# Hybrid encoder block on one core: first weight load moved to ScalarE's queue, transposes of the identity ahead of the first products, last output tile in two halves

## The chip, the core and the metric

The kernel runs on one core of one Trainium2 chip. TensorE (PE) multiplies, VectorE (DVE) and ScalarE (ACT) work on SBUF and PSUM, GpSimd (POOL) on SBUF only; transfers between HBM and SBUF are issued by SyncE (SP) or by ScalarE on queues of their own. The metric is device microseconds of one execution. Three runs of the kernel before gave 1689.59, 1690.15 and 1693.16 us, median 1690.15.

## What is computed

One encoder layer on two sequences, 2048 tokens and 256 tokens, model width 1024, in fp32. Both are laid end to end as 2304 tokens, 18 tiles of 128.

```
hdn  = rmsnorm(x, norm_pre)
proj = hdn @ w_in                # conv branch, q_lat (384), kv_lat (256), k_pe (32), gates
conv = b_gate * short_conv(c_gate * u) * silu(z_conv)
q    = rmsnorm(q_lat) @ w_uq ; k, v = rmsnorm(kv_lat) @ w_ukv ; rope on part of q and k
attn = softmax(q k^T) v * silu(z_attn)        # 8 heads, no mask
out  = concat(conv, attn) @ w_out
y    = x + rmsnorm(out, norm_post)
```

## The kernel before

Products are made exact enough by splitting each operand into a rounded part (hi) and a rest (lo) and by adding three products, hi hi, hi lo and lo hi (`mm3`, lines 91 to 93). ScalarE makes the rounded part (`split`, line 68; `form`, line 141 for the input), VectorE the rest (lines 69 and 142).

Phase 1 (`phase1`) projects the input. Its first step, lines 316 to 325, brings in the first 384 tokens of x, transposed, and the weights of the latents, in eight slices k of 128 input features each. SyncE issues all of these loads, in program order: x slice 0, the norm's gains g_pre, weights 0, x slice 1, weights 1, x slices 2 and 3 in one transfer, weights 2, weights 3, and so on. For each slice ScalarE scales and rounds x (line 141, `hdn_hi`) and rounds the weights (line 68, `wl_hi`), and VectorE forms `hdn_lo` and `wl_lo`. Then `latents` (line 176) runs over k and, for the first call, over two tiles of 128 tokens: per slice 12 products into four PSUM tiles, six of 384 columns (`pq`) and six of 288 (`pk`). Further tiles, the tokens' norms (`norm_x`) and the other projections follow (`etile`, line 242). In phase 1 the program's planner orders the instructions of an engine from its own costs and due times; from the second phase on the order on PE, DVE, ACT and POOL is the order in which they are written (`manual_schedule`, line 1027).

Ahead of phase 1, line 995 runs one small ScalarE instruction, `ready`, so that ScalarE's table load comes early. The identity matrix is made on GpSimd (line 989); PE uses it to transpose (lines 170 and 223).

Phase 2 makes queries, keys and values from the latents; the attention follows (`Attention`), one head pair and 512 queries at a time. Phase 4 (`Phase4`) is the output projection, one tile of 128 tokens after another in the order 16, 17, 0 to 15. `load` issues the loads of a tile two tiles ahead, `split` cuts it one tile ahead, and `run` (line 950) multiplies it: for each half of 512 columns 16 products with the hi part (line 959) and 8 with the lo part (line 961), all into one PSUM tile of 1024 columns, two banks (`g.wide`, two buffers). When both halves are done, this follows for the whole width:

```
nc.scalar.activation(junk, o, AF.Square, accum_out=sq[:, 0:1])
nc.vector.tensor_tensor(yt, o, g.post, op=ALU.mult)
rstd(g, sq[:, 1:2], sq[:, 0:1], D)
nc.vector.scalar_tensor_tensor(yt, yt, sq[:, 1:2], xt, op0=ALU.mult, op1=ALU.add)
nc.sync.dma_start(self.y[i * P : (i + 1) * P], yt)
```

Both read the same PSUM tile; in the trace the VectorE product of line 967 starts when ScalarE has ended the square of line 966. `rstd` (line 96) is two small GpSimd instructions, lines 99 and 100. The tiles `yt`, `o_cut` and the attention's `p` share a ring of six buffers (tag "p"); `g.narrow` gives PSUM tiles of 512 columns, one bank, and is what the attention uses under the tags "m" and "o".

Of the kernel before, what the change touches and what calls it, by code (L numbers as in the profile page):

```python
# [10 lines left out]
F32 = mybir.dt.float32  # L11
F32R = mybir.dt.float32r
# [3 lines left out]
AF = mybir.ActivationFunctionType  # L16
ALU = mybir.AluOpType
# [4 lines left out]
P = 128  # L22
D = 1024
# [10 lines left out]
LW = QL + KL + ROPE  # L34
CW = 512
EPS = 1e-6
# [23 lines left out]
def f(ap):  # L60
    return ap.bitcast(F32)


def split(nc, hi, lo, src, scale=None):

    whole = f(hi) if hi.dtype == F32R else hi
    if scale is None:
        nc.scalar.activation(hi, src, AF.Copy)
        nc.vector.tensor_tensor(lo, src, whole, op=ALU.subtract)
    else:  # L70
        nc.scalar.activation(hi, src, AF.Copy, scale=scale)
        nc.vector.scalar_tensor_tensor(lo, src, scale, whole, op0=ALU.mult, op1=ALU.subtract)
# [30 lines left out]
def phase1(g, x, x_t, w_e, w_lat, npre, convw, open_phase2):  # L103

    nc, tc = g.nc, g.tc
    with ExitStack() as ctx:
        px = ctx.enter_context(tc.tile_pool(name="p1x", bufs=3, reuse_waits="tile"))
        pl = ctx.enter_context(tc.tile_pool(name="p1l", bufs=2, reuse_waits="tile"))
        pb = ctx.enter_context(tc.tile_pool(name="p1b", bufs=2, reuse_waits="tile"))
        ps = ctx.enter_context(tc.tile_pool(name="p1ps", bufs=2, space=PSUM, reuse_waits="tile"))  # L110
# [5 lines left out]
        wl_hi = pw.tile([P, 8, LW], F32R, name="wl_hi")  # L116
        wl_lo = pw.tile([P, 8, LW], F32R, name="wl_lo")
# [11 lines left out]
        def fetch_t(c, ks):  # L129
            if c not in turned:  # L130
                turned[c] = pw.tile([P, 8, CH], F32, tag="xt", bufs=1, name=f"xt{c}")
                hdn[c] = (
                    px.tile([P, 8, CH], F32R, tag="hdn_hi", bufs=3, name=f"hdn_hi{c}"),
                    px.tile([P, 8, CH], F32R, tag="hdn_lo", bufs=3, name=f"hdn_lo{c}"),
                )
            nc.sync.dma_start(turned[c][:, ks], x_t[:, ks, c * CH : (c + 1) * CH])
# [158 lines left out]
        def conv(hf, j, ci):  # L295
# [17 lines left out]
                nc.gpsimd.tensor_tensor(ys, ys, gt[:, gb : gb + n], op=ALU.mult)  # L313
            nc.sync.dma_start(g.mix[j * P : (j + 1) * P, lo_t:hi_t], y[:, : hi_t - lo_t])

        fetch_t(0, slice(0, 1))
        nc.sync.dma_start(g_pre, npre)
        for k in range(8):
            if k == 1 or k and k % 2 == 0:
                fetch_t(0, slice(k, k + 1 + (k > 1)))  # L320
            wt = pb.tile([P, 8, P], F32R if k % 3 else F32, tag=("w32", "w_hi", "w_lo")[k % 3], name=f"wl{k}")
            wt = f(wt.rearrange("p k e -> p (k e)")[:, :LW])
            nc.sync.dma_start(wt, w_lat[:, k, :])
            form(0, [k])
            split(nc, wl_hi[:, k, :], wl_lo[:, k, :], wt)
        for i in range(3):
            fetch_x(i)
            norm_x(i)
# [3 lines left out]
        n = 0  # L332
        for hf in range(2):
            pend = []
            for c in range(3 * hf, 3 * hf + 3):
                ahead = c + 1 < 3 * hf + 3
# [21 lines left out]
            for j in range(5):  # L358
                if j < 4:
                    edge(hf, j, True)  # L360
                for e in range(4):
                    if n + 1 < 20 * (hf + 1):
                        _, j2, e2 = seq[n + 1]
# [559 lines left out]
class Phase4:  # L923
# [23 lines left out]
        eng = nc.vector if i == T // P - 2 else nc.gpsimd  # L947
        eng.tensor_tensor(ml, m, f(mh), op=ALU.subtract)  # L948

    def run(self, i, ahead):  # L950
        g, nc = self.g, self.g.nc
        _, xt, mh, ml = self.ready.pop(i)
        hi, lo = self.wo
        o = g.wide(f"out{i}")
        for b in range(2):
            w = slice(b * 512, (b + 1) * 512)
            for k in range(8):
                for wk in (hi, lo):
                    nc.tensor.matmul(o[:, w], mh[:, k, :], wk[k // 2][:, k % 2, w], start=k == 0 and wk is hi, stop=False)  # L959
            for k in range(8):  # L960
                nc.tensor.matmul(o[:, w], ml[:, k, :], hi[k // 2][:, k % 2, w], start=False, stop=k == 7)  # L961
        ahead()
        yt = self.at.ps.tile([P, D], F32, tag="p", bufs=6, name=f"yt{i}")
        junk = self.at.ps.tile([P, D], F32, tag="acc", bufs=2, name=f"junko{i}")
        sq = self.at.ps.tile([P, 2], F32, tag="sqo", bufs=2, name=f"sqo{i}")
        nc.scalar.activation(junk, o, AF.Square, accum_out=sq[:, 0:1])  # L966
        nc.vector.tensor_tensor(yt, o, g.post, op=ALU.mult)  # L967
        rstd(g, sq[:, 1:2], sq[:, 0:1], D)
        nc.vector.scalar_tensor_tensor(yt, yt, sq[:, 1:2], xt, op0=ALU.mult, op1=ALU.add)  # L969
        nc.sync.dma_start(self.y[i * P : (i + 1) * P], yt)  # L970


@with_exitstack
def tile_encoder(ctx, tc, x, x_t, w_e, w_lat, w_uq, w_uk, w_uv, w_out, convw, npre, qg, kvg, npost, table, y):
    nc = tc.nc
    g = Ctx()
    g.nc, g.tc = nc, tc
    dram = ctx.enter_context(tc.tile_pool(name="scratch", bufs=1, space=DRAM))
    cpool = ctx.enter_context(tc.tile_pool(name="const", bufs=1))
# [11 lines left out]
    g.exps = cpool.tile([P, 2], F32, name="exps")  # L991
    g.mhalf = cpool.tile([P, 10], F32, name="mhalf")
    nc.gpsimd.memset(g.mhalf, -0.5)

    nc.scalar.activation(cpool.tile([P, 10], F32, name="ready"), g.mhalf, AF.Copy)

    p2 = Phase2(g, table)
    phase1(g, x, x_t, w_e, w_lat, npre, convw, lambda *pools: p2.open(w_uq, w_uk, w_uv, w_lat, npre, qg, kvg, *pools))
# [25 lines left out]
    last = len(p2.chunks) - 1  # L1024
# [45 lines left out]
    p4 = Phase4(g, at, x, (wo[:4], wo[4:]), y)  # L1070
    periods = H * KT
    for p in range(periods):
        at.steps(p)
        for s in (2 * p, 2 * p + 1):
            k, i = divmod(s - 8, 28)
# [5 lines left out]
    tiles = [16, 17, *range(16)]  # L1081
# [4 lines left out]
    n = 2 * H - 1  # L1086
    rest = at.finish(n, n // 4, slice(n % 4 * QB, (n % 4 + 1) * QB))
    for n, i in enumerate(tiles):

        def ahead():  # L1090
            if n + 1 < len(tiles):
                p4.split(tiles[n + 1])
            if n + 2 < len(tiles):
                p4.load(tiles[n + 2])

        p4.run(i, ahead)
        if n < 2:
            for _ in range(4):
                next(rest, None)
# [48 lines left out]
```

## Time and profile before

| what | value |
| --- | --- |
| median of three runs | 1690.15 us |
| the profiled execution, its own time | 1692.56 us |
| its span, first to last instruction | 1690.6 us |
| PE busy | 1647.5 us, 97% of the span |
| DVE, ACT, POOL busy | 750.2, 581.6, 878.5 us |
| granted TensorE clock, mean | 0.994 |

The time of an execution is the span and something around it. Busy times are sums over an engine's instructions; an idle engine costs time only where the end waits for it. PE is the engine whose work fills the span, so one looks for the places where PE stands still, and then for what it waited for there.

### The profile page before, as it was taken

The numbers are of one execution on the slowest core, as the hardware profiler recorded it, in microseconds if no ns is written. First come the engines' busy times: TensorE is split into PE (matmuls) and PEld (weight loads), VectorE is DVE, ScalarE is ACT, GpSimd is POOL, SyncE is SP. The second block draws the span as 40 slices with busy tenths as digits, with TensorE's granted clock in tenths as the row PEclk, the third lists the DMA queues.
The fourth block names the chain that finished last, engine by engine and source line by source line (L and its number), as shares of the span: only waits on it lengthen the run. The fifth ranks groups of instructions, "written<-read, shape, count | busy, mean of one in ns | idle before, by whom it ended". The sixth has DMA issues, their size and how long they took to land. (4 is left out here: it accounts for less than half of the span.)

```text
span 1690.6 us, 22364 instructions
## 1 busy us (share of the span) xinstructions
PE 1647.5 (97%) x8870; PEld 1115.8 (66%) x8870; DVE 750.2 (44%) x1125; ACT 581.6 (34%) x804; POOL 878.5 (52%) x637
## 2 busy tenths in 40 slices
PE   8999999999999999978999999999999999999998
PEld 8999999999999997556333333333333333378886
DVE  4333332423474222337556665666666666132122
ACT  7521111452222122411444444444444444512211
POOL 3321221033342112145788988989899898942222
PEclk9999999999999999989999999999999999999999
DMA  8921112364324116378011131113111210034443
GB/s 292 273 87 60 52 52 83 112 165 118 114 94 137 55 62 167 106 194 214 13 32 32 44 85 41 44 32 94 31 45 32 69 44 13 26 105 144 149 141 109
DMA packets 141741, 158.97 MB, mean 94 GB/s; under 512 B 33842, under 2 KB 118116, under 8 KB 141636
## 3 DMA queue, kind: packets, MB, share of 16 engines
q1 hardware_dynamic: 122916, 148.11, 29.3%
q10 hardware_dynamic: 18720, 9.44, 1.9%
q8 instruction: 69, 1.13, 0.3%
q14 instruction: 36, 0.29, 0.1%
HBM read 109.72 MB, written 41.89 MB: 90 GB/s over the span
## 5 line engine op out<-in xcount | busy, mean ns | idle before, releaser
L809 POOL TENSOR_TENSOR acc<-acc,p 128x1024 f32<-128x1024 f32 x224 | 527.9, 2357 | 60.6 <-ACT p L799 50.5
L753 DVE TENSOR_REDUCE mx<-m 128x1 f32<-128x512 f32 x512 | 337.7, 691 | 237.2 <-PE m L752 237.1
L799 ACT ACTIVATE p<-s,exps 128x1024 f32<-128x1024 f32 x256 | 271.4, 1111 | 348.2 <-PE s L794 348.2
L91 PE MATMUL o<-hdn_hi,whi 128*128 128x384 f32 x960 | 323.5, 337 | 0.0
L92 PE MATMUL o<-hdn_lo,whi 128*128 128x384 f32 x960 | 322.7, 336 | 0.0
L93 PE MATMUL o<-hdn_hi,wlo 128*128 128x384 f32 x960 | 322.6, 336 | 0.0
L789 PE MATMUL s<-q,k 128*128 128x512 f16 x1024 | 302.7, 381 | 1.0 <-ACT p L799 1.0
L920 PE MATMUL o<-p,v 128*64 128x512 f32 x1024 | 247.7, 605 | 0.0
L789 PEld LDWEIGHTS <-k 128*128 128x128 f16 x1024 | 90.7, 98 | 190.8 <-issue 101.4
L752 PE MATMUL m<-k,q 96*128 96x512 f16 x512 | 195.4, 382 | 14.4 <-DVE mx L753 8.7
L91 PEld LDWEIGHTS o<-hdn_hi,whi 128*128 128x128 f32 x960 | 180.5, 188 | 0.5
L92 PEld LDWEIGHTS o<-hdn_lo,whi 128*128 128x128 f32 x960 | 180.5, 188 | 0.0
L93 PEld LDWEIGHTS o<-hdn_hi,wlo 128*128 128x128 f32 x960 | 180.5, 188 | 0.0
L920 PEld LDWEIGHTS o<-p,v 128*64 128x64 f32 x1024 | 62.2, 136 | 127.5 <-issue 127.0
L959 PE MATMUL out<-wo,o_cut 128*128 128x512 f32 x576 | 140.4, 396 | 0.0
L959 PEld LDWEIGHTS out<-wo,o_cut 128*128 128x128 f32 x576 | 108.0, 188 | 27.7 <-issue 0.8
L948 POOL TENSOR_TENSOR o_cut<-o_raw,o_cut 128x1024 fp32r<-128x1024 f32 x17 | 40.8, 2399 | 118.3 <-ACT o_cut L945 118.3
L279 POOL TENSOR_TENSOR gt<-gt,z 128x384 f32<-128x384 f32 x24 | 28.7, 1197 | 141.1 <-ACT z L278 141.1
L236 ACT ACTIVATE whi<-w 128x1024 fp32r<-128x1024 f32 x40 | 42.2, 1058 | 172.8 <-PE o L92 159.6
L752 PEld LDWEIGHTS <-q 96*128 96x128 f16 x512 | 49.6, 97 | 63.9 <-issue 6.2
L967 DVE TENSOR_TENSOR yt<-out,g_post 128x1024 f32<-128x1024 f32 x18 | 22.0, 1224 | 150.7 <-ACT junko L966 141.7
L271 POOL TENSOR_TENSOR cu<-cu,rb 128x384 f32<-128x384 f32 (+2 forms) x28 | 27.5, 987 | 112.4 <-DVE cu L270 112.4
(230 smaller groups left out, 2016.4 us busy)
## 6 DMA issues: line engine op xcount, KB each, us to landing
w<-in_w_e_dram SPq DMA_DIRECT2D x40, 512.0 KB, 3.5
x<-in_x_dram SPq DMA_DIRECT2D x18, 512.0 KB, 6.8
o_raw<-mix_s SPq DMA_DIRECT2D x18, 512.0 KB, 4.8
o_raw<-in_x_dram SPq DMA_DIRECT2D x18, 512.0 KB, 5.6
out_dram<-yt SPq DMA_DIRECT2D x18, 512.0 KB, 6.2
q<-qn_s SPq DMA_DIRECT2D x64, 128.0 KB, 2.7
xt<-in_x_t_dram SPq DMA_DIRECT2D x5, 1536.0 KB, 8.3
k<-kn_s SPq DMA_DIRECT2D x12, 512.0 KB, 7.1
```

The lines of the kernel that those rows point to most:

```text
L91: nc.tensor.matmul(out, sh, mh, start=first and i == 0, stop=False)
L92: nc.tensor.matmul(out, sh, ml, start=False, stop=False)
L93: nc.tensor.matmul(out, sl, mh, start=False, stop=last and i == n - 1)
L236: nc.scalar.activation(hi, w, AF.Copy)
L752: nc.tensor.matmul(m, q[:DQK, i, 2, b * P : (b + 1) * P], k[:DQK, i, 1, c * 512 : (c + 1) * 512], start=True, stop=True)
L753: nc.vector.reduce_max(mx[:, u, c : c + 1], m, axis=AX.X)
L789: nc.tensor.matmul(o, k[:, ki, x, ks], q[:, qi, x, :], start=x == 0, stop=False)
L799: nc.scalar.activation(p, o, AF.Exp, scale=g.exps[:, 0:1])
L809: nc.gpsimd.tensor_tensor(self.acc[key], self.acc[key], first, op=ALU.add)
L920: nc.tensor.matmul(self.o[n][i * DV : (i + 1) * DV], g.v[:, kt, h * DV : (h + 1) * DV], p[:, i * QB : (i + 1) * QB], start=kt == 0, stop=k ...
L948: eng.tensor_tensor(ml, m, f(mh), op=ALU.subtract)
L959: nc.tensor.matmul(o[:, w], mh[:, k, :], wk[k // 2][:, k % 2, w], start=k == 0 and wk is hi, stop=False)
```

## The change

Three edits. In phase 1 the load of weight slice 0 is issued by ScalarE's queue, as its first instruction, ahead of SyncE's loads; the other seven stay on SyncE. The `ready` instruction moves from ahead of phase 1 to behind that issue, and eight PE transposes of the identity into two rotating PSUM tiles are added ahead of the first products. In phase 4 the last tile in order (tile 15) is computed in two PSUM tiles of 512 columns, each with its own square, product with `g.post` and, at the end, its own final VectorE instruction and store, the first half by SyncE, the second by ScalarE. In that tile the epsilon is added to half 0's sum, and half 1's sum, half 0's and the factor 1/1024 go into one GpSimd instruction. For every tile, `yt`, `junk` and `sq` are allocated ahead of the products, and `sq` is three columns wide.

```
--- before.py
+++ after.py
@@ -313,16 +313,29 @@
                 nc.gpsimd.tensor_tensor(ys, ys, gt[:, gb : gb + n], op=ALU.mult)
             nc.sync.dma_start(g.mix[j * P : (j + 1) * P, lo_t:hi_t], y[:, : hi_t - lo_t])
+
+        wts = {}
+
+        def fetch_wl(k, queue):
+            wt = pb.tile([P, 8, P], F32R if k % 3 else F32, tag=("w32", "w_hi", "w_lo")[k % 3], name=f"wl{k}")
+            wts[k] = f(wt.rearrange("p k e -> p (k e)")[:, :LW])
+            queue.dma_start(wts[k], w_lat[:, k, :])
+
+        fetch_wl(0, nc.scalar)
         fetch_t(0, slice(0, 1))
         nc.sync.dma_start(g_pre, npre)
+
+        nc.scalar.activation(pl.tile([P, 10], F32, name="ready", bufs=1), g.mhalf, AF.Copy)
+        for i in range(8):
+            turn = ps.tile([P, 3, P], F32, tag="tl", name=f"turn{i}")[:, 0]
+            nc.tensor.transpose(turn, g.ident, g.ident)
         for k in range(8):
             if k == 1 or k and k % 2 == 0:
                 fetch_t(0, slice(k, k + 1 + (k > 1)))
-            wt = pb.tile([P, 8, P], F32R if k % 3 else F32, tag=("w32", "w_hi", "w_lo")[k % 3], name=f"wl{k}")
-            wt = f(wt.rearrange("p k e -> p (k e)")[:, :LW])
-            nc.sync.dma_start(wt, w_lat[:, k, :])
+            if k:
+                fetch_wl(k, nc.sync)
             form(0, [k])
-            split(nc, wl_hi[:, k, :], wl_lo[:, k, :], wt)
+            split(nc, wl_hi[:, k, :], wl_lo[:, k, :], wts.pop(k))
         for i in range(3):
             fetch_x(i)
             norm_x(i)
@@ -947,27 +960,50 @@
         eng = nc.vector if i == T // P - 2 else nc.gpsimd
         eng.tensor_tensor(ml, m, f(mh), op=ALU.subtract)
-    def run(self, i, ahead):
-        g, nc = self.g, self.g.nc
+    def products(self, o, b, mh, ml):
+
+        nc = self.g.nc
+        hi, lo = self.wo
+        w = slice(b * 512, (b + 1) * 512)
+        for k in range(8):
+            for wk in (hi, lo):
+                nc.tensor.matmul(o, mh[:, k, :], wk[k // 2][:, k % 2, w], start=k == 0 and wk is hi, stop=False)
+        for k in range(8):
+            nc.tensor.matmul(o, ml[:, k, :], hi[k // 2][:, k % 2, w], start=False, stop=k == 7)
+
+    def run(self, i, ahead, last):
+        g, nc, ps = self.g, self.g.nc, self.at.ps
         _, xt, mh, ml = self.ready.pop(i)
-        hi, lo = self.wo
+        yt = ps.tile([P, D], F32, tag="p", bufs=6, name=f"yt{i}")
+        junk = ps.tile([P, D], F32, tag="acc", bufs=2, name=f"junko{i}")
+        sq = ps.tile([P, 3], F32, tag="sqo", bufs=2, name=f"sqo{i}")
+        rows = self.y[i * P : (i + 1) * P]
+        if last:
+
+            for b in range(2):
+                w = slice(b * 512, (b + 1) * 512)
+                o = g.narrow(f"out{i}_{b}", "mo"[b])
+                self.products(o, b, mh, ml)
+                nc.scalar.activation(junk[:, w], o, AF.Square, accum_out=sq[:, b : b + 1])
+                nc.vector.tensor_tensor(yt[:, w], o, g.post[:, w], op=ALU.mult)
+                if b == 0:
+                    nc.gpsimd.tensor_scalar(sq[:, 0:1], sq[:, 0:1], 1.0, D * EPS, op0=ALU.mult, op1=ALU.add)
+            nc.gpsimd.tensor_scalar(sq[:, 2:3], sq[:, 1:2], sq[:, 0:1], 1.0 / D, op0=ALU.add, op1=ALU.mult)
+            nc.gpsimd.tensor_tensor(sq[:, 2:3], sq[:, 2:3], g.mhalf[:, :1], op=ALU.pow)
+            for b, queue in enumerate((nc.sync, nc.scalar)):
+                w = slice(b * 512, (b + 1) * 512)
+                nc.vector.scalar_tensor_tensor(yt[:, w], yt[:, w], sq[:, 2:3], xt[:, w], op0=ALU.mult, op1=ALU.add)
+                queue.dma_start(rows[:, w], yt[:, w])
+            return
         o = g.wide(f"out{i}")
         for b in range(2):
-            w = slice(b * 512, (b + 1) * 512)
-            for k in range(8):
-                for wk in (hi, lo):
-                    nc.tensor.matmul(o[:, w], mh[:, k, :], wk[k // 2][:, k % 2, w], start=k == 0 and wk is hi, stop=False)
-            for k in range(8):
-                nc.tensor.matmul(o[:, w], ml[:, k, :], hi[k // 2][:, k % 2, w], start=False, stop=k == 7)
+            self.products(o[:, b * 512 : (b + 1) * 512], b, mh, ml)
         ahead()
-        yt = self.at.ps.tile([P, D], F32, tag="p", bufs=6, name=f"yt{i}")
-        junk = self.at.ps.tile([P, D], F32, tag="acc", bufs=2, name=f"junko{i}")
-        sq = self.at.ps.tile([P, 2], F32, tag="sqo", bufs=2, name=f"sqo{i}")
         nc.scalar.activation(junk, o, AF.Square, accum_out=sq[:, 0:1])
         nc.vector.tensor_tensor(yt, o, g.post, op=ALU.mult)
         rstd(g, sq[:, 1:2], sq[:, 0:1], D)
         nc.vector.scalar_tensor_tensor(yt, yt, sq[:, 1:2], xt, op0=ALU.mult, op1=ALU.add)
-        nc.sync.dma_start(self.y[i * P : (i + 1) * P], yt)
+        nc.sync.dma_start(rows, yt)
 @with_exitstack
@@ -992,8 +1028,6 @@
     g.mhalf = cpool.tile([P, 10], F32, name="mhalf")
     nc.gpsimd.memset(g.mhalf, -0.5)
-    nc.scalar.activation(cpool.tile([P, 10], F32, name="ready"), g.mhalf, AF.Copy)
-
     p2 = Phase2(g, table)
     phase1(g, x, x_t, w_e, w_lat, npre, convw, lambda *pools: p2.open(w_uq, w_uk, w_uv, w_lat, npre, qg, kvg, *pools))
     pool = lambda name, **kw: ctx.enter_context(tc.tile_pool(name=name, reuse_waits="tile", **kw))
@@ -1093,7 +1127,7 @@
             if n + 2 < len(tiles):
                 p4.load(tiles[n + 2])
-        p4.run(i, ahead)
+        p4.run(i, ahead, n + 1 == len(tiles))
         if n < 2:
             for _ in range(4):
                 next(rest, None)
```

## Rows read from the trace of the kernel before

**Rows 1.** Page, part 1: each engine's busy us (share of the span) xinstructions

```profile
PE 1647.5 (97%) x8870; PEld 1115.8 (66%) x8870; DVE 750.2 (44%) x1125; ACT 581.6 (34%) x804; POOL 878.5 (52%) x637
```

**Rows 2.** PE's waits: waiter, what it waited for, us in total, times, longest

```profile
PE qr L91 <- DMA lt_q<-lat_s: 6.2, 1, 6.2
PE pq L91 <- ACT wl_hi L68: 6.0, 1, 6.0
```

**Rows 3.** Timeline, first 12 us: start, us, engine, line, operation, idle before it

```profile
1.07 0.29 POOL masks.py:199 TENSOR_SCALAR_AFFINE_SELECT ident<-ident 128x128 f32<-128x128 f32 x1
1.18 0.42 SPq L317 DMA_DIRECT2D g_pre<-in_npre_dram  x1
1.64 0.43 SPq L323 DMA_DIRECT2D wl<-in_w_lat_dram  x1
...
3.44 0.61 ACT L141 ACTIVATE hdn_hi<-xt,g_pre 128x384 fp32r<-128x384 f32 x1 [1.22 <-DMA g_pre<-in_npre_dram]
...
5.19 0.76 ACT L68 ACTIVATE wl_hi<-wl 128x672 fp32r<-128x672 f32 x1 [1.13 <-DMA wl<-in_w_lat_dram]
...
6.00 0.69 PE L91 MATMUL pq<-wl_hi,hdn_hi 128*128 128x384 f32 x1 [6.00 <-ACT wl_hi L68]
...
8.99 1.12 ACT L141 ACTIVATE hdn_hi<-xt,g_pre 128x384 fp32r<-128x384 f32 x2 [1.41 <-DMA xt<-in_x_t_dram]
...
9.54 0.51 PE L91 MATMUL pq<-wl_hi,hdn_hi 128*128 128x384 f32 x1
...
10.07 0.34 PE L93 MATMUL pq<-wl_hi,hdn_lo 128*128 128x384 f32 x1
...
10.80 1.64 DVE L69 TENSOR_TENSOR wl_lo<-wl,wl_hi 128x672 fp32r<-128x672 f32 x2
...
11.74 0.42 PE L92 MATMUL pq<-wl_lo,hdn_hi 128*128 128x384 f32 x1
```

**Rows 4.** Windows: us, busy us of each engine, granted clock, DMA share, GB/s

```profile
2.50:4.00 1.50, 0.00 (x0) 0.00 (x0) 0.00 (x0) 0.56 (x1) 0.00 (x0) 1.00 0.79 176
4.00:5.50 1.50, 0.00 (x0) 0.00 (x0) 0.62 (x1) 0.37 (x2) 0.00 (x0) 1.00 1.02 371
```

**Rows 5.** The identity's users: count, ns min/median/max, first and last start us

```profile
L223 PE MATMUL tk<-ident,kpl x18: 270/272/273, 37.9 to 417.7; 128*32 128x128 f32 x18
```

**Rows 6.** Timeline of the last output tile, from PE's last eight products

```profile
1681.17 2.03 PE L961 MATMUL out<-wo,o_cut 128*128 128x512 f32 x8
1683.29 1.02 ACT L966 ACTIVATE junko<-out 128x1024 f32<-128x1024 f32 x1 [10.09 <-issue]
1684.21 0.19 ACT L966 ACTIVATION_READ_ACCUMULATOR junko<-out 128x1 f32 x1
1684.44 1.22 DVE L967 TENSOR_TENSOR yt<-out,g_post 128x1024 f32<-128x1024 f32 x1 [8.60 <-ACT junko L966]
...
1684.77 0.54 POOL L100 TENSOR_TENSOR sqo<-sqo,mhalf 128x1 f32<-128x1 f32 x1
1685.75 1.28 DVE L969 SCALAR_TENSOR_TENSOR yt<-yt,sqo,o_raw 128x1024 f32<-128x1024 f32 x1
```

**Rows 7.** Timeline of SyncE's queue after 1682 us: the last store's issue

```profile
1687.06 0.33 SPq L970 DMA_DIRECT2D out_dram<-yt  x1
```

**Rows 8.** Groups by shape, 512 columns from PSUM: busy us, mean ns, idle before

```profile
L820 ACT ACTIVATE rsum<-r 128x512 f32<-128x512 f32 x16 | 9.6, 597 | 11.5 <-PE r L818 11.5
...
L828 DVE TENSOR_TENSOR res<-o,gate 128x512 f32<-128x512 f32 x16 | 11.1, 692 | 48.0 <-POOL gate L825 48.0
```

**Rows 9.** DMA issues after 1685 us: KB each, median us from issue to landing

```profile
out_dram<-yt SPq DMA_DIRECT2D x1, 512.0 KB, 2.6
```

**Rows 10.** DMA issues of the whole span: stores of 128 rows of 2 KB

```profile
mix_s<-res SPq DMA_DIRECT2D x16, 256.0 KB, 2.0
```

**Rows 11.** DMA issues of the whole span: stores on ScalarE's queue

```profile
qn_s<-sq ACTq DMA_DIRECT2D x9, 512.0 KB, 5.6
```

**Rows 12.** Windows: a stretch in the projection stage with a lower granted clock

```profile
740.00:760.00 20.00, 13.97 (x87) 9.98 (x88) 5.64 (x10) 2.17 (x3) 8.29 (x7) 0.74 0.63 181
```

## The prediction

> **What bounds the kernel now.** The page's first part comes first: TensorE (PE) is busy 97% of the span [rows 1], so a change counts only where PE stands still or comes after the last product. Then PE's waits [rows 2]: one of the largest is 6.0 us, ahead of the very first product; the 6.2 us one lies in the projection stage, on data that this stage itself makes, so it moves along with whatever comes before. The change touches the first stretch and the one after the last product. Behind it PE has no row of waiting that comes from the start, so I let what is won there travel to the end.
>
> In the first stretch [rows 3] follow one input slice k = 0..7 at a time: two loads (x, then weights), ScalarE rounds each, VectorE forms the rests, PE multiplies. ScalarE sat idle 1.13 us for the first weights and began at 5.19; PE began at 6.00. Later it sat idle 1.41 us for x slices 2 and 3, until 8.99; VectorE had the weight rests of 2 and 3 from 10.80 on, about 11.62 for slice 2 (half of 1.64), and the first product that needs them starts at 11.74 and takes 0.42 instead of the 0.34 of its shape. So PE arrives at slice 2 only just before its data. That is the important reading: a PE that starts earlier, or runs faster in slices 0 and 1, waits there.
>
> In the last stretch [rows 6, 7] PE ends at 1683.20 (1681.17 + 2.03); the square on ScalarE, its accumulator, the product with g.post, the final VectorE instruction and the store follow each other, and the span ends at 1690.6: 7.4 us with PE idle.
>
> **The change, part by part.**
>
> *First weights on ScalarE's queue.* The issue at 1.64 leaves SP; each SP load behind it moves up by the spacing of two issues, 1.64 - 1.18 = 0.46 us [rows 3]. On ScalarE the issue stands ahead of the table load and the `ready` instruction; at SP's 0.43 it pushes them to about 2.7, and ScalarE waits for g_pre until 3.44 anyway, so that costs nothing; without that cover it would cost 0.43. What is won is how much earlier slices 2 and 3 land, since they hold PE next: 0.46, plus the 0.08 that PE lost at slice 2, about 0.5 us. How the byte stream reacts is not shown, so it is bounded. From 2.5 to 4.0 us the DMAs moved 176 GB/s, right after that 371 [rows 4]. If the early issue fills this hole completely, 1.5 x (371 - 176) / 371 = 0.79 us are won, 0.87 with the 0.08. If the engines, already 0.79 busy there, only swap one load for another, it is nothing. A loss is excluded as far as I see: the bytes ahead of slice 2 are the same ones. I take 0.5, nearest to the issue spacing, and keep 0 and 0.87.
>
> The row speaks for 0.79, since the engines moved less than half of what they could. The Trainium skill ("DMA: Bandwidth & Descriptors", section "Issuing engines are not separate DMA queues") says that transfers issued by different engines interleave on the same 16 DMA engines, and that issuing from several saves only the sequencer's issue time. By that rule the end of 0.79 falls away and the sum below stays as it is; no stretch of this trace has two queues loading weights at once.
>
> *Transposes of the identity ahead of the first products.* Eight, on an otherwise idle PE, from about 1.4 us (the identity's last instruction on GpSimd). One transpose took 0.27 us at the full clock [rows 5]; doubled for the half clock and laid end to end, 8 x 0.54 = 4.3 us, until 5.7. The first product could come at about 5.2 instead of 6.0, so they could delay it to 5.7, which is still early enough for slice 2. What they may bring is the clock: the granted clock prints 1.00 from the start, yet a 384-column product took 0.51 us at 9.54 and 0.34 at 10.07 [rows 3], so I read 1.2 GHz for PE's first 4 us of work and 2.4 after it. Twelve products ran before 9.54; at 0.17 each that is 2.0 us at most, in front of the wait at slice 2, which swallows it: with data 0.46 earlier, PE gets 0.54 whether it comes to slice 2 early or very early. So I put the transposes at zero, with slice 2 as the cover; if the loads came much earlier they would be worth up to the difference.
>
> Rows 3 can't say whether transposes raise the clock. The Trainium skill ("TensorE: Matmul & The Clock Gate", Part 4, "PE-mode transpose") says that the full clock does not engage for them, since they don't count as busy in the same way. By that rule the start is worth some 0.4 instead of 0.5, since a cold PE starting at 5.7 comes 0.1 late to slice 2 (6.00 to 11.74 now took 5.7 us), and the sum would be 1.5 instead of 1.6.
>
> *Moved tiles.* yt, junk and sq are now taken ahead of the products in every output tile. yt still follows the yt of two tiles before in its ring of six, and the loads follow those of two tiles before, which they wait for anyway through the raw buffers: nothing.
>
> *The last tile in halves.* Each half has its own PSUM bank. Half 0 ends about 5.6 us before PE does, so its square, product and the small GpSimd step lie under half 1's products. For half 1 the chain is: square on 512 columns 0.60 [rows 8] from 1683.29, its accumulator read out from 1683.79 to 1683.98 (overlapping by 0.10 as now); then the two GpSimd steps, 0.91 from the end of the accumulator to the end of the power (1684.40 to 1685.31 now [rows 6]), to about 1684.9. VectorE's product, 0.69 for 512 columns [rows 8], runs beside it from 1684.0 to 1684.7. So GpSimd now releases the last instruction, where the long product did before. Then two final instructions on VectorE: 1.28 for 1024 columns; with the slope of (1.22 - 0.69)/512 columns one half is 0.75. With 0.1 for the handoff: 1685.0 to 1685.75, and 1686.5. The last store is issued at 1686.5 instead of 1687.06, and is 256 KB: such a store took 2.0 us to land [rows 10], the last one of 512 KB 2.6 [rows 9]. So 0.55 + 0.6, about 1.1 us. Nothing is queued behind the new issue on ScalarE. Upper end 1.4 (handoff and the pointer operand cost nothing, the two stores overlap well); lower end 0, where the store on ScalarE's queue takes 1.1 us longer to land.
>
> **Sum.** 0.5 + 1.1 = 1.6 us. The profiled execution took 1692.56 with a span of 1690.6 (1.96 around it); it would become 1690.96. The median of three, 1690.15, is 2.41 lower than the profiled execution; the same 1.6 off it gives 1688.55, rounded to 1688.6.
>
> **Rivals.**
> - *The loads only swap places.* Start worth 0, end 1.1: 1689.05. For it: the engines are 0.79 busy in the hole. Against: their rate there is under half.
> - *Both ends at their best.* 0.87 + 1.4 = 2.3: 1687.9. The hole is filled, and the clock is up when slice 2 is there. This is also the case in which the transposes pay.
> - *The last store lands late (slower).* Place: after 1686.5. Stores on ScalarE's queue took a median of 5.6 us to land [rows 11], though larger in number of packets and beside other traffic. At 5.6 instead of 2.0 the end is 3.6 later: 1690.15 - 1.6 + 3.6 = 1692.15, slower than before; it decides from a landing of 3.6 us on (2.0 + 1.6). Against it: at the end nothing else is on the DMAs.
> - *Another clock dip in the middle.* Between 740 and 760 the granted clock was 0.74 with 13.97 us of PE work [rows 12], after PE's wait of 6.2 us. One more such dip costs (1 - 0.74) x 13.97 = 3.6 us, one less gives as much: 1692.2 or 1685.0. The four executions shown of the same program already span 1689.59 to 1693.16, 3.57 us, about that price; a shift of half a microsecond can land in either.
> - *The change does nothing at the end* (the halves wait for each other in another way) is inside the bounds of the forecast: 1689.65.
>
> **How the numbers follow.** Forecast 0.45 (its own range 1687.7 to 1689.7), loads swap 0.2, both best 0.14, late store 0.07, another dip 0.14. The range takes in the first three with the scatter of runs, and most of the dip upward: 1686.4 to 1691.4. About 0.2%, 3.4 us, is what a measurement of this kernel can tell from no change. Faster by more needs a time under 1686.77: the best case with luck, or a dip less: 0.08. Slower by more needs one over 1693.53: 0.05. The rest, 0.87, is the same.
>
> **What would show it.** In the changed trace: the weights' first ScalarE instruction before 5.19; PE's first product between 5.1 and 5.8; x slices 2 and 3 about 0.46 before 8.99; the second product of slice 2 about 0.5 before 11.74, with a wait ahead of it if the clock was up. At the end, PE's last product to the end of the span 6.3 us instead of 7.4, GpSimd's power as what VectorE waits for, and the last store landing in 2.0. The forecast is wrong if slice 2's products start at 11.7 again, if PE shows a new wait between 12 and 640 us, if the store on ScalarE's queue takes over 3 us, or if the stretch from 640 to 860 us changes by more than 1 us.

## The result, and the profile after

The change makes the kernel slower: a median of 1702.36 us over six runs (1698.16 to 1703.24), beside 1692.8 over six runs of the kernel before (1689.59 to 1694.47). The ratio is 1.0055, with a 95% interval of 1.004 to 1.0071. The forecast of 1688.6 and its whole range (up to 1691.4) lie below that. The prediction gave a clear loss a chance of 0.05, and it came by a way that none of its rivals names.

The profiled execution after took 1703.24 us with a span of 1701.4, 10.8 more than before. The page's first part shows where to look:

```profile
PE 1660.4 (98%) x8878; PEld 1127.1 (66%) x8878; DVE 752.2 (44%) x1127; ACT 582.1 (34%) x806; POOL 880.4 (52%) x638
```

Beside [rows 1] PE has eight instructions more, the transposes, and is busy 12.9 us longer. So PE did not come to stand still; it worked longer on the same products. PE's waits in the changed kernel say the same, since they answer to [rows 2] with nearly the same sizes and have no new large row:

```profile
PE qr L91 <- DMA lt_q<-lat_s: 6.4, 1, 6.4
PE pq L91 <- ACT hdn_hi L141: 5.9, 1, 5.9
```

Starts of the same instructions in both traces cut the 10.8 us into stages. The second projection (`etile`: 2880 products `o<-hdn`, the inputs moving past the weights) began at 75.53 us before and at 77.44 after, and its last product at 645.10 and 656.76. The output products began at 1478.65 and 1490.49. From PE's end to the span's end it is 7.40 us before and 6.39 after. So between these two executions the start lost 1.9 us, the stretch of the second projection 9.75, all between there and PE's end 0.2, and the end won 1.0.

**The start.** The timeline of the changed kernel, in the columns of [rows 3]:

```profile
0.72 0.39 ACTq L322 DMA_DIRECT2D wl<-in_w_lat_dram  x1
...
4.63 0.76 ACT L68 ACTIVATE wl_hi<-wl 128x672 fp32r<-128x672 f32 x1 [1.97 <-DMA wl<-in_w_lat_dram]
...
5.30 1.11 ACT L141 ACTIVATE hdn_hi<-xt,g_pre 128x384 fp32r<-128x384 f32 x2
...
5.95 0.69 PE L91 MATMUL pq<-wl_hi,hdn_hi 128*128 128x384 f32 x1 [5.95 <-ACT hdn_hi L141]
...
7.46 1.12 ACT L141 ACTIVATE hdn_hi<-xt,g_pre 128x384 fp32r<-128x384 f32 x2 [0.29 <-DMA xt<-in_x_t_dram]
...
9.75 2.23 PE L331 MATMUL turn<-ident 128*128 128x128 f32 x8
...
11.63 0.62 PE L91 MATMUL pq<-wl_hi,hdn_hi 128*128 128x384 f32 x1
...
12.09 0.34 PE L92 MATMUL pq<-wl_lo,hdn_hi 128*128 128x384 f32 x1
```

The weights are rounded at 4.63 instead of 5.19, but the first product starts at 5.95 instead of 6.00, because x slice 0 now comes second on ScalarE. The eight transposes stand *behind* the twelve products of slice 0, from 9.75 to 11.63, although the program text has them ahead: in phase 1 the planner orders PE. And the first product at the short duration of 0.34 us comes at 12.09, where it came at 10.07 before.

The loads: windows of the changed kernel, columns as in [rows 4], then DMA issues of its first 6 us (KB each, median us from issue to landing), and last the rows of g_pre and of x slice 0 in that view of the kernel before.

```profile
2.50:4.00 1.50, 0.00 (x0) 0.00 (x0) 0.00 (x0) 0.15 (x1) 0.00 (x0) 1.00 0.91 326
4.00:5.50 1.50, 0.00 (x0) 0.00 (x0) 0.08 (x1) 0.87 (x2) 0.00 (x0) 1.00 1.04 335
```

```profile
wl<-in_w_lat_dram ACTq DMA_DIRECT2D x1, 336.0 KB, 3.9
xt<-in_x_t_dram SPq DMA_DIRECT2D x1, 192.0 KB, 4.1
g_pre<-in_npre_dram SPq DMA_DIRECT2D x1, 4.0 KB, 3.8
```

```profile
g_pre<-in_npre_dram SPq DMA_DIRECT2D x1, 4.0 KB, 2.2
xt<-in_x_t_dram SPq DMA_DIRECT2D x1, 192.0 KB, 2.5
```

The hole was filled, 326 instead of 176 GB/s, and x slices 2 and 3 were rounded from 7.46 on instead of 8.99. Still the first product got almost nothing. Its three loads traded places: the weights came earlier, but x slice 0, issued at 0.72 in both kernels, took 4.1 us instead of 2.5, and the 4 KB of gains, issued at 1.18 in both, took 3.8 instead of 2.2. They landed at about 4.6, 4.8 and 5.0; then ScalarE rounds the weights first and x slice 0 from 5.30 on. The Trainium skill ("DMA: Bandwidth & Descriptors", section "Issuing engines are not separate DMA queues") says that transfers of different issuers interleave on the same engines; these rows agree, and show the price for the small load.

**The second projection.** Windows inside it, before and then after (busy us and instructions of PE, PEld, DVE, ACT, POOL; granted clock, DMA share, GB/s):

```profile
200.00:340.00 140.00, 140.00 (x820) 140.00 (x819) 48.10 (x69) 34.10 (x58) 22.65 (x29) 1.00 0.23 79
400.00:600.00 200.00, 199.31 (x1180) 198.26 (x1179) 96.18 (x181) 44.26 (x66) 65.44 (x69) 1.00 0.33 105
```

```profile
200.00:340.00 140.00, 140.00 (x800) 140.00 (x799) 45.85 (x65) 29.34 (x46) 21.69 (x24) 1.00 0.23 78
400.00:600.00 200.00, 199.35 (x1159) 198.31 (x1158) 95.08 (x178) 43.74 (x68) 60.90 (x69) 1.00 0.34 104
```

PE is as busy in both, at a granted clock of 1.00, yet it does 800 products instead of 820, and 1159 instead of 1180. From start to start of neighbouring products (gaps over 0.4 us left out) the mean is 173.7 ns before and 177.0 after: 3.3 ns x 2880 = 9.5 us. That is nearly the whole loss.

**The end** of the changed kernel, against [rows 6, 7], and its two last stores, against [rows 9]:

```profile
1693.03 2.02 PE L972 MATMUL out<-wo,o_cut 128*128 128x512 f32 x8
1695.09 0.60 ACT L987 ACTIVATE junko<-out 128x512 f32<-128x512 f32 x1 [4.86 <-PE out L972]
...
1696.30 0.54 POOL L992 TENSOR_TENSOR sqo<-sqo,mhalf 128x1 f32<-128x1 f32 x1
1696.87 1.42 DVE L995 SCALAR_TENSOR_TENSOR yt<-yt,sqo,o_raw 128x512 f32<-128x512 f32 x2 [0.37 <-POOL sqo L992]
...
1698.32 0.36 ACTq L996 DMA_DIRECT2D out_dram<-yt  x1
```

```profile
out_dram<-yt ACTq DMA_DIRECT2D x1, 256.0 KB, 2.0
```

GpSimd's power now releases the last VectorE instructions, 1.82 us behind PE's end (1695.05); the last store is issued 3.27 us behind it and lands in 2.0.

### The profile page after: what moved, and what is told of

Same layout as the page of the kernel before. It is cut to its first block, busy times and chain, and to the rows that moved or that the text cites. A ratio compares the mean times of both kernels' runs of the same rounds, so it can differ in the third digit from the quotient of the medians.

```text
span 1701.4 us, 22382 instructions
## 1 busy us (share of the span) xinstructions
PE 1660.4 (98%) x8878; PEld 1127.1 (66%) x8878; DVE 752.2 (44%) x1127; ACT 582.1 (34%) x806; POOL 880.4 (52%) x638
```

## Experiments

### What made the second projection slower

The `ready` tile of ten floats (40 bytes, 64 as laid out) left the constant pool, which lies ahead of most other tiles in SBUF, for a pool of phase 1. Everything that follows the constant pool thereby lies 64 bytes lower in a partition: the inputs `hdn`, for one. The weights `whi` and `wlo` lie behind phase 1's pool and keep their place. The first pair of runs moves only that tile, in the one kernel back and in the other out.

```
a_ready_const: after.py
-        nc.scalar.activation(pl.tile([P, 10], F32, name="ready", bufs=1), g.mhalf, AF.Copy)
+        nc.scalar.activation(g.ready, g.mhalf, AF.Copy)
...
+    g.ready = cpool.tile([P, 10], F32, name="ready")
b_ready_moved: before.py
-    nc.scalar.activation(cpool.tile([P, 10], F32, name="ready"), g.mhalf, AF.Copy)
+        nc.scalar.activation(pl.tile([P, 10], F32, name="ready", bufs=1), g.mhalf, AF.Copy)
```

> The changed kernel, with the 40-byte tile of the `ready` instruction back in the constant pool, so that every SBUF address after it is the one of the kernel before (the input tiles hdn 64 bytes higher than in the changed kernel); nothing else differs, the PSUM banks and the eight transposes stay as changed. Theory A (the address of the moving operand hdn sets the pace of the 2880 products of line 91 to 93 in the second projection): spacing from 177.0 back to 173.4 to 173.7 ns, that stretch 9.5 us shorter, time about 9.5 us under the changed kernel, within 3 us of the kernel before. Theory B (the other PSUM banks that the transposes leave to the products): spacing stays at 177, time as changed, some 10 us over before. In both the first stretch still carries the transposes' 2 us and the end its 1 us gain.

> The kernel before, with only the `ready` tile taken from the first phase's pool instead of the constant pool: hdn and all that follows lies 64 bytes lower, PSUM banks, order of loads and products as before. Theory A: spacing 177.0 ns, the stretch 9.5 us longer, time about 9.5 us over before. Theory B: spacing 173.7, time as before within 2 us.

Measured: with the tile back in place the whole change stands at a ratio of 0.9993 (0.9982 to 1.0005); the move alone, with nothing else of the change, at 1.0065 (1.0045 to 1.0085). Spacing in the second projection is 173.7 ns in the first and 177.0 in the second. The same window, of the kernel before with the tile moved:

```profile
400.00:600.00 200.00, 199.35 (x1159) 198.31 (x1158) 93.58 (x177) 42.85 (x64) 61.95 (x69) 1.00 0.34 104
```

The 1159 products are those of the changed kernel. The first run keeps the other PSUM banks that the transposes leave to the products, so these are not the cause. So the slower pace is the moved tile's, whole. Next: is it the inputs' own place or their place against the weights?

```
c_weights_moved: after.py; i_w64: before.py (with 32, 48, 64 floats: i_w128, i_w192, i_w256)
+        pad = pb.tile([P, 16], F32, name="pad", bufs=1)
+        nc.gpsimd.memset(pad[:, :16], 0.0)
         g_pre = pl.tile([P, 8], F32, name="g_pre", bufs=1)
h_ready32, h_ready128: before.py, n = 8 or 32
-    nc.scalar.activation(cpool.tile([P, 10], F32, name="ready"), g.mhalf, AF.Copy)
+    nc.scalar.activation(cpool.tile([P, n], F32, name="ready")[:, :8], g.mhalf[:, :8], AF.Copy)
```

> The changed kernel with a 64-byte tile ahead of the pool that holds the weights of the second projection: their addresses rise by 64, hdn stays where the change put it. If the distance between weights and input counts (modulo 128 bytes it is then as in the kernel before): spacing 173.4 to 173.7 ns and some 9.5 us less than the changed kernel. If the input's own address counts: 177.0 ns, time as changed. In between: both count.

> The kernel before with the weights alone moved up by 64 bytes (96 modulo 128), hdn where it was (64 modulo 128): the distance differs from the kernel before by 64, as it does in the changed kernel. Distance alone: 177 ns and some 9.5 us slower. The input's own place alone: 173.4, time as before.

> The kernel before with the `ready` tile cut to 32 bytes, so that the input hdn and the weights w_hi and w_lo both lie 32 bytes lower (hdn at 32 modulo 128, weights at 0); their distance is that of the kernel before. If only the distance between the two operands sets the pace: 173.4 ns in both halves of the second projection. If the input's own place matters: another spacing, between 173.4 and 177.

> The kernel before with the `ready` tile widened to 128 bytes: hdn and weights both 64 bytes higher (hdn at 0 modulo 128, as in the changed kernel, weights at 96, as in c_weights_moved); same distance as in the kernel before. Distance alone: 173.4 in both halves. hdn at 0 modulo 128 alone: 177 in both. As c_weights_moved did: 176.4 in the first half of the second projection and 173.4 in the second; then the place, and not the transposes, makes that difference.

Moving the weights alone by 64 bytes (i_w64), with the inputs where they were, gives 177.0 ns and 1696.96 us, beside 1691.94 for the kernel before on the same chip. Moving inputs and weights together, by 32 bytes down or 64 up, leaves 173.7 ns. So the pace hangs on where the two lie against each other. Shifting the weights up by 64 bytes as well (c) did not restore it; that makes the distance 128 bytes less than before, and gave 176.5 ns in the first half of the stage and 173.9 in the second, where the kernel before has 173.5 and 173.9 (1694.85 us, before's median beside it 1689.96). Windows of that run:

```profile
200.00:340.00 140.00, 140.00 (x801) 140.00 (x800) 46.59 (x66) 30.36 (x48) 21.74 (x24) 1.00 0.23 78
400.00:600.00 200.00, 199.31 (x1180) 198.26 (x1179) 94.78 (x181) 44.23 (x67) 62.44 (x70) 1.00 0.34 105
```

A surprise stood in h_ready32, at 1682.05 us beside 1691.94. Its second projection is as before, but in the output projection, where `o_cut` moves with the constant pool and `wo` does not, PE does more. The same window, before and then h_ready32:

```profile
1500.00:1660.00 160.00, 160.00 (x688) 128.79 (x687) 36.69 (x30) 31.52 (x43) 45.58 (x44) 1.00 0.44 144
```

```profile
1500.00:1660.00 160.00, 160.00 (x708) 132.48 (x707) 39.13 (x32) 30.80 (x43) 45.89 (x45) 1.00 0.45 146
```

Spacing of the 512-column products is 227.1 ns against 233.7: 6.6 x 864 = 5.7 us. With 64 bytes of shift either way it was 233.7 (after) and 234.7 (h_ready128). The distance between operands matters there too.

More distances, by moving the weights alone; the last three start from the version j below, whose inputs and weights lie 32 bytes lower. The runs c, h and i, and d, e and g below, are single executions, and their times scatter by more than the pace explains (i_w128 1695.04, i_w192 1691.81, i_w256 1691.07 us, beside 1690.36 for the kernel before); what is compared is the spacing in their traces.

> The kernel before with the weights of the second projection 128 bytes higher, inputs unmoved. Theory A, the pace hangs on the distance between the operands modulo 256 bytes: the distance is that of the run in which inputs and weights were moved apart by 128 bytes, so 176.4 ns in the first half and 173.4 in the second, mean 175.2, 4.3 us more in the second projection than before. Theory B, modulo 128: as before, 173.7. Output products 233.7 ns on both, their operands do not move.

> The kernel before with the weights of the second projection 192 bytes higher, inputs unmoved. Theory A (distance modulo 256) has seen no run at this distance: between 173.4 and 177 ns, no number of its own. Theory B (modulo 128): as the run with the weights moved by 64 bytes, 177.0 ns, 9.5 us more.

> The kernel before with the weights of the second projection 256 bytes higher, inputs unmoved. Theories A and B (distance modulo 256 or 128): as before, mean 173.7 ns. Theory C, the place of the weights itself counts and no pattern repeats: some other pace, between 173.4 and 177 ns or outside.

```
l_w32, l_w96, l_w160: j_halves_ready32, n = 8, 24, 40
+        pad = pb.tile([P, n], F32, name="pad", bufs=1)
+        nc.gpsimd.memset(pad[:, :8], 0.0)
         g_pre = pl.tile([P, 8], F32, name="g_pre", bufs=1)
```

> The version with halves and a 32-byte `ready` tile, with the weights of the second projection 32 bytes higher, so that inputs minus weights is 128 modulo 256. Theory A, an even multiple of 32 is faster as in the output products (2.8% there): some 168.8 ns, 14 us less in the second projection, ratio to before near 0.988. Theory B, only 64 bytes off is slow and everything else runs at 173.7: 173.7 ns, ratio 0.996.

> As the run before it, weights 96 bytes higher, inputs minus weights 64 modulo 256. Theory A: some 168.8 ns, ratio near 0.988. Theory B: between the slow 177.0 at 96 and the 173.7 to 175.2 at 32: 174 to 177 ns, ratio 0.997 to 1.002.

> As the run before it, weights 160 bytes higher, inputs minus weights 0 modulo 256, the distance that the output products have where they are fast. Theory A: some 168.8 ns, ratio near 0.988. Theory B: 173.7 to 175 ns, ratio 0.996 to 0.999. Theory C, only 0 is fast: 168.8 ns here, and not in the two runs before it.

Mean spacing in the second projection, by the place of inputs minus weights modulo 256 bytes (places as laid out in the compiled kernels: before, `hdn_hi0` at 17216 and `whi0` at 140704):

```
  0   l_w160                          173.7 ns
 32   c_weights_moved, i_w128         175.2, 173.9
 64   l_w96                           173.7
 96   after, b_ready_moved, i_w64     177.0, 177.0, 177.0
128   l_w32                           176.2
160   before, a, h_ready32, h_ready128, j, i_w256   173.7
224   i_w192                          173.7
```

i_w256 is back at the value of before, so a shift of 256 changes nothing, and i_w192 at 173.7 against i_w64 at 177.0 rules out a pattern of 128. That an even multiple of 32 bytes is faster (theory A of the last three) fell: 64 and 0 are no faster than 160, and 128 is slow:

```profile
400.00:600.00 200.00, 199.35 (x1166) 198.30 (x1165) 93.77 (x180) 43.03 (x65) 60.59 (x64) 1.00 0.34 105
```

(l_w32, ratio 0.9994, 0.9984 to 1.0003: its slow second projection eats what its output products and halves win.) Distance alone is not the whole law either: at 32 two kernels differ, 175.2 and 173.9, with other absolute places. These two means are mixtures. The stage runs through 40 weight tiles, the buffers of the inputs lie a multiple of 256 bytes from one another, and so do those of the weights, so the distance modulo 256 is the same for each. Yet c runs its weight tiles 3 to 20 at the slow pace of the changed kernel and the others at that of before, and i_w128 only the 1st, 22nd and 27th at the slow one. So at this distance both paces occur, in one execution and at the same places. What in the chip makes some distances slow, and what chooses there, stays open. The Trainium skill ("SBUF — State Buffer", section "Who interferes with whom") gives PE two independent read ports, for the moving operand and for weight loads, and says that PE never waits on anyone. Read so, no distance should matter; the runs differ from that by 1.9% (177.0 against 173.7), and the measurement decides.

### What the start lost

```
f_turn_first: a_ready_const
+            last_turn = nc.tensor.transpose(turn, g.ident, g.ident)
...
+                        with tc.issue_after(last_turn.ins):
+                            done = latents(tiles)
d_no_turn: a_ready_const
-        for i in range(8):
-            turn = ps.tile([P, 3, P], F32, tag="tl", name=f"turn{i}")[:, 0]
-            nc.tensor.transpose(turn, g.ident, g.ident)
g_x_before_w: f_turn_first
+                made[c, k] = nc.scalar.activation(
...
+            with tc.issue_after(made[0, k].ins):
                 split(nc, wl_hi[:, k, :], wl_lo[:, k, :], wts.pop(k))
```

> The changed kernel with the old addresses (as a_ready_const), and the eight transposes put in front of the first products on TensorE by an order edge, which is what the change says it does. If my prediction's slice-2 argument holds: transposes from about 1.4 us on, first product between 5.5 and 6.0, no transposes later, the second projection starts about 0.5 us before the 75.53 of the kernel before (2.4 us before the changed kernel's 77.44), and the time is about 1.5 us under before. If transposes raise the clock, 384-column products take 0.34 us from the first one on and a wait of about 1 us stands ahead of slice 2; if they don't, the first products take 0.5 us as before.

> The changed kernel with `ready` in its old pool and the eight transposes left out; the weights' load stays on ScalarE's queue. Theory A, the transposes are what the start lost: PE held 2.2 us by them behind slice 0 and they give no clock, so the first 12 products run straight on, the second projection begins 1.4 to 2.2 us before 76.96 (at 74.8 to 75.6), the span is about 1686. Theory B, the order of ScalarE's work is what the start lost (the wait for a rounded x slice near 34 us): the 2.2 us only move into that wait, the second projection begins at 76.7 to 77.3 again, the span stays near 1687.5. On either theory the products of the second projection stay at 173.7 ns.

> The transposes first on PE (as in the run with the transposes first) and, in each slice, ScalarE's rounding of x ahead of its rounding of the weights. Theory A, ScalarE's order made the wait of 1.3 to 1.45 us near 34 us: with the old order it is gone, the second projection begins at 75.5 to 76.0 instead of 77.26, the first product near 5.5. Theory B, the wait comes from the loads: it stays, and the second projection begins at 77.0 to 77.5. Products of the second projection at 173.7 ns on either.

Without the transposes (d, 1689.6 us beside 1692.79) the second projection begins at 75.55, against 76.96 with them (a) and 75.53 before. Taken as they stand, these three traces say that the transposes cost 1.4 us and that the earlier weights were worth nothing. But the start scatters: in the 13 traces of kernels whose first loads and products are ordered as before, the second projection begins between 74.80 (l_w160) and 76.43 (e_halves). With the transposes behind slice 0 it begins at 77.44, 77.01 (c), 76.96 (a) and, with the best addresses, 75.91 (k, below), where the kernels with the same `ready` tile and the old start have 74.80 to 75.73. What is certain is that the transposes hold PE for 1.3 us (k) to 1.9 us (the changed kernel) and that no wait behind them takes it back; the price of 1.4 is that of one pair. The timeline of d:

```profile
7.56 1.12 ACT L141 ACTIVATE hdn_hi<-xt,g_pre 128x384 fp32r<-128x384 f32 x2 [0.52 <-DMA xt<-in_x_t_dram]
...
9.37 1.68 DVE L69 TENSOR_TENSOR wl_lo<-wl,wl_hi 128x672 fp32r<-128x672 f32 x2
...
10.62 0.29 PE L91 MATMUL pk<-wl_hi,hdn_hi 128*128 128x288 f32 x1
...
11.95 0.34 PE L91 MATMUL pq<-wl_hi,hdn_hi 128*128 128x384 f32 x1
```

Slice 2's data are 1.4 us earlier than before, its first product at 11.95 is later (11.56 before), and no wait stands ahead of it. Not the data but PE's slow first products set that time: full pace (0.29 for 288 columns) comes at 10.62, where it came at 10.07 before.

With the transposes held first (f, ratio 0.9993, 0.9983 to 1.0002), its timeline shows what they do for the clock:

```profile
1.42 2.29 PE L331 MATMUL turn<-ident 128*128 128x128 f32 x8 [1.42 <-POOL ident masks.py:199]
6.10 0.69 PE L91 MATMUL pq<-wl_hi,hdn_hi 128*128 128x384 f32 x1 [2.39 <-ACT hdn_hi L141]
...
8.86 0.52 PE L93 MATMUL pq<-wl_hi,hdn_lo 128*128 128x384 f32 x1
...
10.15 0.34 PE L92 MATMUL pq<-wl_lo,hdn_hi 128*128 128x384 f32 x1
```

The first products still last 0.52 us and 0.34 only from 10.15 on, 1.2 and 2.4 GHz as I read them, since the granted clock prints 1.00 throughout. From the first product to full pace it is 4.1 us here and 3.6 in g, which has the transposes first too; it is 4.7 in d, and in the 13 traces with the old order anything from 3.0 (h_ready128) to 6.1 (h_ready32), without any transpose. The 6.1 of the changed kernel lies at the edge of that. So whatever transposes ahead or between the products change in the time to full pace, it does not stand out from this scatter. The Trainium skill ("TensorE: Matmul & The Clock Gate", Part 4, "PE-mode transpose") says the full clock does not engage for them. The products of f and g, slow after eight transposes and an idle stretch, agree with that; but in k full pace came ahead of the transposes and they ran at it, and in c it came while only transposes ran, behind twelve products. Rows of k, then durations of the transposes (ns, least, median, most) in the changed kernel and in k:

```profile
9.25 0.29 PE L92 MATMUL pk<-wl_lo,hdn_hi 128*128 128x288 f32 x1
...
9.52 1.54 PE L331 MATMUL turn<-ident 128*128 128x128 f32 x8
10.81 0.42 PE L91 MATMUL pq<-wl_hi,hdn_hi 128*128 128x384 f32 x1
```

```profile
L331 PE MATMUL turn<-ident x8: 415/421/475, 9.7 to 11.6; 128*128 128x128 f32 x8
```

```profile
L331 PE MATMUL turn<-ident x8: 271/272/328, 9.5 to 10.8; 128*128 128x128 f32 x8
```

Then f loses 1.3 us of its own, at a wait that neither before nor a has, and g, where ScalarE rounds x ahead of the weights as before, keeps it. PE's waits in g, up to 80 us:

```profile
PE pq L91 <- ACT wl_hi L68: 2.4, 1, 2.4
...
PE pq L91 <- ACT hdn_hi L141: 1.4, 1, 1.4
```

Both begin the second projection at 77.3. In g's timeline the wait ends at 35.60, for a rounded slice which ScalarE begins at 34.93, behind its latents' work (lines 200, 201, 71) and norms; before, the same four slices begin at 33.17. So both theories of g fell: the loads are innocent and so is ScalarE's first order; the planner, given one more order edge, queued ScalarE otherwise 25 us later. g also shows the price of the early weights for x: slice 0, here first again, is rounded at 4.76 instead of 3.44, having waited for g_pre:

```profile
ACT hdn_hi L141 <- DMA g_pre<-in_npre_dram: 2.1, 1, 2.1
```

### The halves alone, and a better kernel

e_halves is the kernel before with the change's `products`, `run` and the call with `last`, and nothing at the start. j_halves_ready32 adds h_ready32's edit; k_after_ready32 is a_ready_const with `ready` eight floats wide.

> The kernel before with the last tile in halves (and the moved allocations) and nothing else. From PE's last product's end to the end of the span 6.4 us instead of 7.4 (the changed kernel has 6.4), the second projection at 173.4 ns, the first products at 6.0 and the second projection from 75.5 as before; the moved tiles change nothing. Rival: the moved allocations or the halves cost something before the last tile, and the stretch from 1478 us to PE's end grows over 205.1 us.

> The kernel before with the last tile in halves and the `ready` tile cut from 40 to 32 bytes, nothing at the start. If the pace of the output products follows the distance of their two operands in SBUF: 227 ns instead of 233.7 in 864 products, 5.7 us, and 1.0 us from the halves: ratio to before 0.996 (6.7 us off some 1690). If the earlier single run at 1682.05 was mostly chance in the stretch from 646 to 800 us: output products at 233.7 ns again, ratio 0.9994.

> The whole change, with the `ready` tile back in its old pool and 32 bytes wide. If distance alone sets the pace: second projection at 173.7 ns, output products at 227 ns, 5.7 us under the run with `ready` back in place (ratio 0.9993 there): ratio 0.996. The start, 1.4 us later than before, is in that ratio. If the 32 bytes did not set the pace: 0.9993 again.

e took 1688.06 beside 1691.94, with 6.39 us from PE's end to the span's end as in the changed kernel, 1.0 less than before. (Its first product came at 6.75 and its second projection at 76.43, not at 6.0 and 75.5; in h_ready128, whose start is that of before, the first product came at 6.83: the start's own scatter.) j stands at 0.9964 (0.995 to 0.9978), k at 0.9953 (0.9939 to 0.9968), and l_w96, the same as j with its weights 96 bytes on, at 0.9952 (0.9935 to 0.997) and 1682.18 us: the lowest median of those that ran more than once, though the three intervals overlap; l_w160 stands at 0.9965 (0.9952 to 0.9978). All beat the kernel before by some 6 to 8 us, and the changed kernel by more; 5.7 of it comes by eight bytes less in one tile that nothing reads.

## Why the prediction was wrong

- **"Moved tiles ... nothing"** is the step that failed. The term listed `yt`, `junk` and `sq` and asked who waits for whom. The one tile that counted, `ready`, appears in the prediction only as an instruction on ScalarE; that its pool shifts every tile behind it was not asked. In its place: 64 bytes, 9.5 us, shown by a and b. No rival had it; the likely cases differed at the two ends alone, so the range could not hold it. The test "a new wait between 12 and 640 us" pointed at the right stretch but at the wrong sign of trouble: no wait, but a pace.
- **"Transposes ... from about 1.4 us on ... at zero, with slice 2 as the cover"** failed twice. The planner put them behind slice 0, where they hold PE for 1.3 to 1.9 us (1.4 us in a against d); and the cover did not exist. Their size was off too: the 0.27 us of [rows 5] is a duration at the full clock, and at half pace the duration is 0.42 to 0.48, but they follow each other every 0.27 us. The eight of f took 2.3 us, not 4.3.
- **"PE arrives at slice 2 only just before its data"** was the false reading under the start's 0.5 us. d brought the data 1.4 us earlier and PE came no sooner. PE's slow first products bound that stretch, as d shows; the two happened to meet in [rows 3]. The "first 4 us" at half pace were one draw from 3.0 to 6.1. The sum's 0.5 became about 0 for the weights, as far as the scatter of the start lets one tell.
- "A loss is excluded" was too strong: the bytes ahead of slice 2 are the same, but x slice 0 and the gains, which the first product needs, came 1.6 us later. The rival *the loads only swap places* has the right worth, 0, by luck: for slice 0 they did swap, but slices 2 and 3 came 1.5 us earlier (1.4 in d), more than the upper bound of 0.87 allowed, and PE was not waiting for them.
- **The end, 1.1 us**, was right in mechanism and size: 1.0 measured, with the power 1.8 us behind PE and the store landing in 2.0, both as worked out.
- **Another clock dip** is not the cause here. From the end of the second projection to the first `s` product it is 153.7 us before and 152.6 after. That stretch does scatter, 148.7 in a, but not as the rival has it: PE is busy 131.9 us of it before and 131.5 in a, so what differs is idle time, not the length of the products.
- The start of the changed kernel lost 1.9 us and that of a 1.4. The half microsecond between them is inside the scatter of the start. b, which has the moved tile alone, begins the second projection 0.6 later than before; in its trace full pace comes at 11.89 instead of 10.07 and slice 2's first product 0.9 later. h_ready32 and i_w128, with other addresses, reach full pace as late as b.

## What to carry to other kernels

When an edit moves, adds or drops any tile, compare where the operands of the busiest products lie before and after, and count matmuls in a fixed window at a fixed granted clock: a loss of pace shows in no wait. Where a planner orders instructions, a place in the program text is no order; read it from the trace, and expect an added order edge to reshuffle other engines far behind it. A hole in the loads can be filled at the cost of the loads that the first instruction needs. And a single trace of a start that scatters by 1.6 us can't price an edit of one.

## What was not expected of the hardware

In the runs here the time between fp32 products changes with the distance in SBUF between the two operands: 173.7 to 177.0 ns for 384 columns, 227.1 to 234.7 for 512, with shifts of 32 bytes deciding and a shift of 256 changing nothing in the one case tried. At one distance (32) both paces of the 384-column products occur in one execution. PE is fully busy and its clock fully granted in all of them. PE's time from the first product to full pace varied from 3.0 to 6.1 us between executions with the same order of work at the start.
